# Seven quarter products for the gated up-projections, with weight sums on GpSimd

## The chip, the core and the metric

One core of one Trainium2 chip runs the whole program. Its engines have a queue each: TensorE multiplies and accumulates in PSUM, VectorE, ScalarE and GpSimd work element by element, and SyncE issues the transfers from HBM. The metric is the time of one execution on the device in microseconds; smaller is better.

## The reference

Two transformer blocks follow each other on one sequence of 512 tokens with 1024 features. The second block, which the change concerns, has two layers, and each layer is

```python
x = _layer_norm(alpha * x + 0.5 * _swiglu(x, ffn_w_gu[l, 0], ffn_w_down[l, 0]), ln_g[l, 0], ln_b[l, 0])
mix = _token_mixers(x, ...)            # four attentions side by side
x = _layer_norm(alpha * x + mix, ln_g[l, 1], ln_b[l, 1])
x = _layer_norm(alpha * x + 0.5 * _swiglu(x, ffn_w_gu[l, 1], ffn_w_down[l, 1]), ln_g[l, 2], ln_b[l, 2])

def _swiglu(h, w_gu, w_down):
    gate, up = jnp.split(h @ w_gu, 2, axis=-1)   # 1024 -> 2 x 2816
    return (jax.nn.silu(gate) * up) @ w_down     # 2816 -> 1024
```

All of it is in float32. There are four such feed-forwards, and each has 2816 / 128 = 22 "gated units": 128 gate features with the 128 up features that they multiply.

## The kernel before

Activations lie with features on the partitions: x is eight tiles of 128 features by 512 tokens (names h or x). Every operand of a product is kept as two float32r parts, a high part, which ScalarE rounds, and a low part, which VectorE gets as the difference (split, lines 406 to 409; load_split, lines 386 to 404, for weights that stream in). mm3 (lines 419 to 423) makes one 128x128 block's product as three matmuls: high by high, high by low, low by high.

swiglu works in two halves of 11 units. Of each unit it takes the gate and then the up features: proj loads 128x1024 weights, splits them in two pieces of 512 columns, and mac runs 8 x 3 matmuls over all 512 tokens into one bank. evac (line 853 on) puts SiLU of the gate into sg, multiplies it with the up product and splits the result into mid. After each half eight products over the 11 tiles of mid go down again to 1024 features and are added to x; those of the second half lie in out_norm, which also normalises.

out_norm makes the last two feature blocks by halves of the tokens. The left half's statistics, mean and normalisation run beside the right half's products. The right half's run as self.tail between the first products of the next stage: stats (the reductions, 1/std by GpSimd at line 479, and the subtraction of the mean at line 808, four tiles on VectorE and four on GpSimd), then norm for eight tiles (lines 815 to 822). chunks lets the next stage begin with four sources that take the left half of the tokens alone, so with 256 columns.

The tile framework draws up the order of each engine's queue when the program is built, with priority by program order: a weight split is queued as soon as its buffers come free, ahead of earlier code that still waits. Weights have three raw tiles (tag wr) and two pairs of parts (tags wh, wl). The working banks of PSUM are two each of tags acc, s and t, and one o.

## Time and profile before

| | |
|---|---|
| runs of the kernel, us | 3460.77, 3419.64, 3463.23 (median 3460.77) |
| span of the profiled execution, us | 3418.7 |
| the profiled execution's own time, us | 3419.64 (the run that its span fits, 0.9 around it) |
| TensorE busy | 3343.1 us, 98% |
| VectorE / ScalarE / GpSimd busy | 55% / 41% / 10% |
| mean granted TensorE clock | 0.993 |
| read from HBM | 280.20 MB, 83 GB/s |

A profile row of an engine counts an instruction from its start to its end. Matmuls overlap in the array (one of 512 columns lasts about 395 ns, and the next starts before it ends), so their pace is read from how many fit into a stretch. A window lists an instruction in every stretch that it touches. VectorE's rows overlap a little, too. A granted clock of 1.00 is 2.4 GHz, 0.5 is 1.2 GHz.

### The profile page before, as it was taken

What the parts mean: (1) busy time and instruction counts of PE and PEld (TensorE: products, weight loads), DVE (VectorE), ACT (ScalarE), POOL (GpSimd) and SP (SyncE); (2) the same over time, 40 slices, a digit from 0 to 9 for tenths busy, and PEclk for the clock granted to TensorE, in tenths of its full rate; (3) what the DMA queues carried; (4) which work ended last, traced back from release to release, by engine and by line L of the source; (5) the groups of instructions that cost most, each with busy time, mean ns of one, the idle gap of its engine ahead of it and who ended that gap; (6) DMA issues with size and microseconds to landing.
All of it is one profiled execution on the core that took longest, in us unless ns stands there. A gap on an engine that the chain in (4) does not pass through costs nothing.

```text
span 3418.7 us, 41218 instructions
## 1 busy us (share of the span) xinstructions
PE 3343.1 (98%) x15718; PEld 2681.8 (78%) x15718; DVE 1893.4 (55%) x3378; ACT 1388.7 (41%) x2680; POOL 343.0 (10%) x287
## 2 busy tenths in 40 slices
PE   8999999999999999999999999999999999999998
PEld 6776888887788888888867788888888877788887
DVE  7855564658674655344578843335333467863334
ACT  6322442436342443223466642224222356752233
POOL 3101110113110110000200100002000210010002
PEclk9999999999999999999999999999999999999999
DMA  3211223232223223232312222322232312122322
GB/s 119 88 51 48 88 91 100 89 109 68 87 94 97 93 86 99 88 102 85 108 56 65 67 81 85 101 89 90 86 103 92 112 59 78 33 89 86 105 89 78
DMA packets 105685, 293.35 MB, mean 86 GB/s; under 512 B 20752, under 2 KB 35344, under 8 KB 105232
## 3 DMA queue, kind: packets, MB, share of 16 engines
q1 hardware_dynamic: 105488, 290.73, 26.8%
q8 instruction: 123, 2.02, 0.2%
q14 instruction: 74, 0.61, 0.1%
HBM read 280.20 MB, written 2.62 MB: 83 GB/s over the span
## 4 chain that ended last, share of the span: by engine, by line
PE 84%; DVE 8%; issue 3%; ACT 2%; POOL 1%; DMA 0%; SPq 0%; ACTq 0%; DVEq 0%; POOLq 0%
PE psacc L421 15%; PE psacc L422 15%; PE psacc L423 15%; PE pss L421 5%; PE pss L423 4%; PE pss L422 4%; PE pst L421 4%; PE pst L422 4%; PE pst L423 4%; PE pso L421 2%; PE pso L423 2%; PE pso L422 2%; PE pst L1384 1%; DVE wl L403 1%; PE pso L1394 1%
## 5 line engine op out<-in xcount | busy, mean ns | idle before, releaser
L402 ACT ACTIVATE wh<-wr 128x512 fp32r<-128x512 f32 (+1 forms) x1008 | 587.5, 616 | 1301.3 <-PE psacc L422 452.1
L403 DVE TENSOR_TENSOR wl<-wr,wh 128x512 fp32r<-128x512 f32 (+1 forms) x1008 | 671.7, 692 | 653.0 <-ACT wh L402 643.4
L421 PE MATMUL psacc<-xh,wh 128*128 128x512 f32 (+1 forms) x1800 | 711.3, 396 | 10.4 <-ACT wh L402 7.8
L423 PE MATMUL psacc<-xh,wl 128*128 128x512 f32 (+1 forms) x1800 | 708.3, 394 | 10.0 <-DVE wl L403 10.0
L422 PE MATMUL psacc<-xl,wh 128*128 128x512 f32 (+1 forms) x1800 | 709.1, 394 | 2.8 <-DVE xl L523 2.4
L423 PEld LDWEIGHTS psacc<-xh,wl 128*128 128x128 f32 x1800 | 342.1, 190 | 90.8 <-DVE wl L403 13.0
L421 PEld LDWEIGHTS psacc<-xh,wh 128*128 128x128 f32 x1800 | 341.5, 190 | 91.4 <-ACT wh L402 9.6
L422 PEld LDWEIGHTS psacc<-xl,wh 128*128 128x128 f32 x1800 | 341.9, 190 | 80.7 <-DVE xl L523 5.6
L421 PE MATMUL psacc<-ph,wh 128*128 128x512 f32 x775 | 308.3, 398 | 4.6 <-DVE pl L409 2.0
L423 PE MATMUL psacc<-ph,wl 128*128 128x512 f32 x775 | 307.6, 397 | 2.4 <-DVE wl L403 2.4
L422 PE MATMUL psacc<-pl,wh 128*128 128x512 f32 x775 | 306.7, 396 | 0.1
L421 PEld LDWEIGHTS psacc<-ph,wh 128*128 128x128 f32 x775 | 145.8, 188 | 40.6 <-PE pss L423 2.8
L423 PEld LDWEIGHTS psacc<-ph,wl 128*128 128x128 f32 x775 | 145.9, 188 | 36.5 <-DVE wl L403 2.8
L422 PEld LDWEIGHTS psacc<-pl,wh 128*128 128x128 f32 x775 | 145.9, 188 | 33.8 <-DVE pl L409 0.9
L421 PE MATMUL pst<-xh,wh 128*128 128x512 f32 (+1 forms) x408 | 155.8, 384 | 4.2 <-ACT xh L818 4.2
L422 PE MATMUL pst<-xl,wh 128*128 128x512 f32 (+1 forms) x408 | 156.2, 385 | 0.2 <-DVE xl L819 0.2
L423 PE MATMUL pst<-xh,wl 128*128 128x512 f32 (+1 forms) x408 | 155.4, 383 | 0.0
L421 PE MATMUL pss<-xh,wh 128*128 128x512 f32 x392 | 155.1, 396 | 0.0
L422 PE MATMUL pss<-xl,wh 128*128 128x512 f32 x392 | 155.0, 395 | 0.0
L423 PE MATMUL pss<-xh,wl 128*128 128x512 f32 x392 | 155.0, 395 | 0.0
L577 DVE SCALAR_TENSOR_TENSOR cv<-u,vecs,cv 128x510 f32<-128x510 f32 (+1 forms) x176 | 131.1, 749 | 5.2 <-ACT cv L575 2.3
L586 POOL TENSOR_TENSOR cv<-cv,cv 128x512 f32<-128x512 f32 x44 | 57.3, 1302 | 542.7 <-DVE cv L577 517.6
(434 smaller groups left out, 5473.3 us busy)
## 6 DMA issues: line engine op xcount, KB each, us to landing
wr<-wg SPq DMA_DIRECT2D x176, 512.0 KB, 3.5
wr<-wu SPq DMA_DIRECT2D x88, 512.0 KB, 3.5
wr<-we SPq DMA_DIRECT2D x64, 512.0 KB, 3.5
wr<-wd SPq DMA_DIRECT2D x32, 512.0 KB, 3.4
wr<-we SPq DMA_DIRECT2D x64, 192.0 KB, 2.3
wr<-wi SPq DMA_DIRECT2D x22, 512.0 KB, 3.8
wr<-w_ret SPq DMA_DIRECT2D x16, 512.0 KB, 3.6
wr<-wl_in SPq DMA_DIRECT2D x16, 512.0 KB, 3.6
```

Of the source, the lines that this page charges most:

```text
L402: nc.scalar.activation(hi[:, a:b], raw[:, a:b], AF.Copy)
L403: nc.vector.tensor_tensor(lo[:, a:b], raw[:, a:b], hi[:, a:b].bitcast(F32), op=ALU.subtract)
L421: nc.tensor.matmul(ps, wh, xh, start=start, stop=False)
L422: nc.tensor.matmul(ps, wh, xl, start=False, stop=False)
L423: nc.tensor.matmul(ps, wl, xh, start=False, stop=stop)
L577: nc.vector.scalar_tensor_tensor(out=e[:, s:], in0=u[:, : T - s], scalar=self.v(f"fcw{l}{2 - s}", ch), in1=e[:, s:], op0=ALU.mult, op1=ALU ...
L586: nc.gpsimd.tensor_tensor(gate[:], gate[:], val[:], op=ALU.mult)
L1384: nc.tensor.transpose(pt[:, qb * P : (qb + 1) * P], t[:, kb * P - k0 : (kb + 1) * P - k0], self.ident)
L1394: nc.tensor.matmul(acc[0:64, q], v[:, kb, 0:64], lo[:, q], start=False, stop=False)
```

## The change

Weights and tokens of a unit are cut into quarters: gate and up rows by two halves of the 1024 input features (a11, a12, a21, a22), and x by the same halves of features and by left and right tokens (b11, b12, b21, b22). In place of eight quarter products, seven are formed from sums of quarters. Each is 4 blocks x 3 matmuls of 256 columns (prod), and R and Q accumulate several of them.

- Strassen holds the three quarters of X that are used plain ("11", "21", "22") and four sums of quarters (d, t3, t4, nf). combine makes the sums, for feature tiles j and j + 4 at a time, with four GpSimd operations of 256 columns, and splits them. out_norm's tail calls it in four rounds.
- strassen_w loads the gate and up rows of a unit and forms four sums of 512 columns on GpSimd (p1 to p4); the split is done in pieces of 1024 columns (twice or three times) and one of 512. Its raw sums (tag wc) have two tiles, which combine also uses.
- gated runs a unit's products, shifted against the unit before by the calls of next in swiglu. Evictions: e1, e2, e3 by ScalarE, combinations by VectorE, the product of gate and up by GpSimd.
- The first six units (NFIRST) of a feed-forward run the products "11" and "12" first, on the left tokens alone. Later they load their weights again for the other five products (first=False), and e2 and e3 are then formed by VectorE.
- The 22 units come in parts of 8, 8 and 6 in place of 11 and 11, so down-projections run in three parts.
- normed takes the place of rms_in for the first feed-forward of the block (its X1 is the left half only, and finish makes the rest).
- X's tiles are paired (x4), and new double tiles (xs, six) take over half of the attentions' m tiles. out_norm's late weights lie in wh2 and wl2, or in xs. load_split, weights and mm3 pass tags and a keyword on. Comments are dropped throughout.

```diff
+PARTS = ((0, 8), (8, 16), (16, 22))
+NFIRST = 6
...
+class Strassen:
+    def __init__(self, p):
+        self.p = p
+        self.parts = {n: (p.x4(), p.x4()) for n in ("11", "21", "22")}
+        self.sums = [(p.x4(), p.x4()) if j == 0 else (p.x4("xs"), p.x4("xs")) for j in range(4)]
+    def __getitem__(self, name):
+        if name in self.parts:
+            return [tuple(t[:, j * H : j * H + H] for t in self.parts[name]) for j in range(4)]
+        i = ("d", "t3", "t4", "nf").index(name)
+        return [tuple(t[:, i * H : i * H + H] for t in self.sums[j]) for j in range(4)]
+    def block(self, k, t):
+        name = f"{k // 4 + 1}{t + 1}"
+        return self[name][k % 4] if name in self.parts else None
+    def combine(self, j, x):
+        nc, p = self.p.nc, self.p
+        b11, b12, b21, b22 = (x[k][:, c] for k in (j, j + 4) for c in HALVES)
+        raw = p.pool.tile([P, 2 * T], F32, tag="wc", name=p.nm("wc"), bufs=2)
+        d, t3, t4, f = (raw[:, i * H : i * H + H] for i in range(4))
+        nc.gpsimd.tensor_tensor(t3, b22, b12, op=ALU.subtract)
+        nc.gpsimd.tensor_tensor(f, t3, b11, op=ALU.add)
+        nc.gpsimd.tensor_tensor(d, b11, b12, op=ALU.subtract)
+        nc.gpsimd.tensor_tensor(t4, f, b21, op=ALU.subtract)
+        hi, lo = self.sums[j]
+        n = 3 * H
+        nc.scalar.activation(hi[:, n:], f, AF.Copy, scale=-1.0)
+        nc.vector.scalar_tensor_tensor(
+            out=lo[:, n:], in0=f, scalar=-1.0, in1=hi[:, n:].bitcast(F32), op0=ALU.mult, op1=ALU.subtract
+        )
+        p.split(raw[:, :n], hi[:, :n], lo[:, :n])
...
+            if form == "strassen":
+                for j in range(4):
+                    norm(HALVES[1], f, (j, j + 4))
+                    X.combine(j, x)
+                    yield
+                return
...
+        def finish(bc):
+            for j in range(4):
+                for k in (j, j + 4):
+                    nc.vector.scalar_tensor_tensor(
+                        out=h[k][:], in0=h[k][:], scalar=self.v(gain, k), in1=bc[:], op0=ALU.mult, op1=ALU.mult
+                    )
+                    for t in range(2):
+                        if pair := X.block(k, t):
+                            self.split(h[k][:, t * H : t * H + H], *pair)
+                X.combine(j, h)
+                yield
...
+    def strassen_w(self, sa, sb, first=True):
+        nc = self.nc
+        out = {}
+        def put(names, src, tags, bufs=2, pool=None):
+            n = len(names) * 512
+            hi, lo = ((pool or self.pool).tile([P, n], F32R, tag=t, name=self.nm(t), bufs=bufs) for t in tags)
+            self.split(src, hi[:], lo[:])
+            for i, name in enumerate(names):
+                out[name] = [
+                    (hi[:, c : c + P], lo[:, c : c + P]) for c in range(i * 512, i * 512 + 512, P)
+                ]
+        ra = self.raw(sa, 1024)
+        if first:
+            put(("11", "12"), ra[:], ("wh", "wl"), pool=self.main)
+        if sb is None:
+            return out
+        rb = self.pool.tile([P, 1024], F32, tag="wr2", name=self.nm("wr2"), bufs=2)
+        nc.sync.dma_start(rb[:], sb)
+        a11, a12, a21, a22 = ra[:, :512], ra[:, 512:], rb[:, :512], rb[:, 512:]
+        c1, c2 = (self.pool.tile([P, 1024], F32, tag="wc", name=self.nm("wc"), bufs=2) for _ in range(2))
+        p2, p1, p3, p4 = c1[:, :512], c1[:, 512:], c2[:, :512], c2[:, 512:]
+        nc.gpsimd.tensor_tensor(p1, a21, a22, op=ALU.add)
+        nc.gpsimd.tensor_tensor(p2, p1, a11, op=ALU.add)
+        put(("p2", "p1"), c1[:], ("wh", "wl"), pool=self.main)
+        nc.gpsimd.tensor_tensor(p3, a11, a21, op=ALU.add)
+        nc.gpsimd.tensor_tensor(p4, p2, a12, op=ALU.add)
+        put(("p3", "p4"), c2[:], ("wh2", "wl2"))
+        put(("22",), a22, ("wh3", "wl3"), 1)
+        return out
+    def prod(self, ps, W, X, start):
+        for j in range(4):
+            self.mm3(ps[:, :H], *W[j], *X[j], start and j == 0, j == 3, skip_group_check=True)
+    def scratch(self):
+        return [self.pool.tile([P, T], F32, tag="m", name=self.nm("g"), bufs=self.bufs["m"]) for _ in range(2)]
+    def gated(self, X, srcs, mid, tags, sent=None):
+        nc = self.nc
+        tr, tq, tz = tags
+        gv, hv = sent or self.scratch()
+        g1, g2, e1, n2 = gv[:, :H], gv[:, H:], hv[:, :H], hv[:, H:]
+        silu = lambda t: nc.scalar.activation(t, t, AF.Silu)
+        if sent is None:
+            W = self.strassen_w(*srcs)
+            R = self.pt(tag=next(tr))
+            self.prod(R, W["11"], X["11"], True)
+            nc.scalar.copy(e1, R[:, :H])
+            yield
+            Z = self.pt(tag=next(tz))
+            self.prod(Z, W["12"], X["21"], True)
+            nc.vector.tensor_tensor(g1, e1, Z[:, :H], op=ALU.add)
+            silu(g1)
+            yield
+        else:
+            W = self.strassen_w(*srcs, first=False)
+            R = self.pt(tag=next(tr))
+        e2, e3 = (self.pool.tile([P, H], F32, tag="u", name=self.nm("u"), bufs=3)[:] for _ in range(2))
+        def out(t):
+            if sent is None:
+                nc.scalar.copy(t, R[:, :H])
+            else:
+                nc.vector.tensor_tensor(t, e1, R[:, :H], op=ALU.add)
+        self.prod(R, W["p2"], X["nf"], sent is not None)
+        out(e2)
+        yield
+        Q = self.pt(tag=next(tq))
+        self.prod(Q, W["p1"], X["d"], True)
+        yield
+        self.prod(R, W["p3"], X["t3"], False)
+        out(e3)
+        nc.vector.scalar_tensor_tensor(out=n2, in0=e3, scalar=-1.0, in1=Q[:, :H], op0=ALU.mult, op1=ALU.subtract)
+        yield
+        self.prod(R, W["22"], X["t4"], False)
+        if sent is None:
+            last = R[:, :H]
+        else:
+            nc.vector.tensor_tensor(e1, e1, R[:, :H], op=ALU.add)
+            last = e1
+        nc.vector.scalar_tensor_tensor(out=g1, in0=last, scalar=-1.0, in1=g1, op0=ALU.mult, op1=ALU.mult)
+        yield
+        self.prod(Q, W["p4"], X["22"], False)
+        nc.vector.tensor_tensor(g2, e2, Q[:, :H], op=ALU.add)
+        silu(g2)
+        nc.gpsimd.tensor_tensor(g2, g2, n2, op=ALU.mult)
+        pair = self.xpair("m")
+        self.split(gv[:], pair[0][:], pair[1][:])
+        mid.append(pair)
...
+            if n1:
+                if normed is not None:
+                    X1, X, scale, finish = normed
+                    left, right = X1[:4], X1[4:]
                 else:
+                    left, right = X["11"], X["21"]
+                held = []
+                def done(W, R, gv):
+                    self.prod(R, W["12"], right, False)
+                    if bc is None:
+                        nc.scalar.activation(gv[:, :H], R[:, :H], AF.Silu)
+                    else:
+                        nc.vector.tensor_tensor(gv[:, :H], R[:, :H], bc[:, :H], op=ALU.mult)
+                        nc.scalar.activation(gv[:, :H], gv[:, :H], AF.Silu)
+                for j in range(n1):
+                    W = self.strassen_w(wg[a + j], None)
+                    R = self.pt(tag=next(around))
+                    self.prod(R, W["11"], left, True)
+                    if normed is not None and j == 0:
+                        bc = scale()
+                        self.tail = finish(bc)
+                    gv, hv = self.scratch()
+                    early.append((gv, hv))
+                    if bc is None:
+                        nc.scalar.copy(hv[:, :H], R[:, :H])
+                    else:
+                        nc.vector.tensor_tensor(hv[:, :H], R[:, :H], bc[:, :H], op=ALU.mult)
+                    held.append((W, R, gv))
+                    if j > 0:
+                        done(*held.pop(0))
+                    next(self.tail, None)
+                done(*held.pop(0))
+                for _ in self.tail:
+                    pass
+            before = None
+            for j in range(a, b):
+                sent = early[j - a] if j - a < n1 else None
+                g = self.gated(X, (wg[j], wg[FC + j]), mid, tags, sent)
+                next(g)
+                if before:
+                    next(before)
+                next(g)
+                if before:
+                    next(before, None)
+                for _ in range(1 if sent else 3):
+                    next(g)
+                before = g
+            for _ in before:
+                pass
...
-                    ps = self.proj(I[f"we{l}{s}"][nb][:, : HF * P], mid, HF)
+                    ps = self.proj(I[f"we{l}{s}"][nb][:, a * P : b * P], mid, b - a)
...
-        return self.phase(name, None, m=38, e=6)
+        return self.phase(name, None, m=20)
...
-        return self.phase(name, None, m=24, v=8, pt=4, e=5, y=4, p1=1)
+        return self.phase(name, None, m=12, v=8, pt=4, e=5, y=4, p1=1)
```

## Rows read from the trace of the kernel before

**Rows 1.** The page's first part: busy us (share of the span) and instructions.
```profile
span 3418.7 us, 41218 instructions
PE 3343.1 (98%) x15718; PEld 2681.8 (78%) x15718; DVE 1893.4 (55%) x3378; ACT 1388.7 (41%) x2680; POOL 343.0 (10%) x287
```
**Rows 2.** The page's chain that ended last, shares of the span by engine.
```profile
PE 84%; DVE 8%; issue 3%; ACT 2%; POOL 1%; DMA 0%; SPq 0%; ACTq 0%; DVEq 0%; POOLq 0%
```
**Rows 3.** Windows: steady up-projection, unbroken 256 columns, and a transition between stages.
```profile
core 0: us, PE busy (x) PEld busy (x) DVE busy (x) ACT busy (x) POOL busy (x), PEclk, DMA share, GB/s
1480.00:1580.00 100.00, 100.00 (x430) 80.55 (x430) 44.28 (x70) 30.56 (x53) 0.00 (x0) 1.00 0.29 95
1687.00:1695.00 8.00, 8.00 (x70) 8.00 (x70) 2.08 (x3) 4.61 (x10) 0.00 (x0) 1.00 0.40 131
1965.00:1988.00 23.00, 20.83 (x159) 19.98 (x158) 21.64 (x51) 18.20 (x43) 4.50 (x5) 0.93 0.15 46
```
**Rows 4.** Lines by form, ScalarE and VectorE: busy us, mean ns, idle before.
```profile
L402 ACT ACTIVATE wh<-wr 128x512 fp32r<-128x512 f32 x920 | 541.3, 625 | 1198.0 <-PE psacc L422 410.5 <-issue 404.6 <-PE pss L422 149.2
L408 ACT ACTIVATE ph<-sg 128x512 fp32r<-128x512 f32 x90 | 56.1, 623 | 36.9 <-DVE sg L869 30.3 <-DVE sg L1282 4.4 <-DVE sg L1280 2.1
L774 ACT ACTIVATE sq<-h 128x256 f32<-128x256 f32 x32 | 13.0, 412 | 27.3 <-DVE h L739 27.3
L1450 ACT COPY y<-psacc 128x256 f32<-128x256 f32 x12 | 4.4, 363 | 6.9 <-PE psacc L423 6.9
...
L409 DVE TENSOR_TENSOR pl<-sg,ph 128x512 fp32r<-128x512 f32 x90 | 62.0, 689 | 11.2 <-ACT ph L408 10.2
L409 DVE TENSOR_TENSOR pl<-sg,ph 128x256 fp32r<-128x256 f32 x12 | 5.0, 419 | 2.1 <-ACT ph L408 2.1
L739 DVE SCALAR_TENSOR_TENSOR h<-psacc,h 128x256 f32<-128x256 f32 x14 | 5.8, 416 | 5.5 <-PE psacc L423 5.5
```
**Rows 5.** Lines by form, GpSimd: its commonest operation on 512 columns.
```profile
L586 POOL TENSOR_TENSOR cv<-cv,cv 128x512 f32<-128x512 f32 x44 | 57.3, 1302 | 542.7 <-DVE cv L577 517.6 <-ACT cv L585 25.1
```
**Rows 6.** Line 808 on both engines: ns min/median/max, first and last start us.
```profile
L808 DVE TENSOR_TENSOR h<-h,bc x48: 424/954/987, 1660.0 to 3410.4; 128x256 f32<-128x256 f32 x48
L808 POOL TENSOR_TENSOR h<-h,bc x48: 731/916/981, 1660.2 to 3411.0; 128x256 f32<-128x256 f32 x48
```
**Rows 7.** Timeline: start us, us; two low parts with GpSimd's operation, two without.
```profile
413.58 2.38 DVE L403 TENSOR_TENSOR wl<-wr,wh 128x512 fp32r<-128x512 f32 x2
413.84 1.58 POOL L586 TENSOR_TENSOR cv<-cv,cv 128x512 f32<-128x512 f32 x1 [3.11 <-DVE cv L577]
...
1309.70 1.29 DVE L403 TENSOR_TENSOR wl<-wr,wh 128x512 fp32r<-128x512 f32 x2 [4.76 <-ACT wh L402]
```
**Rows 8.** Timeline of VectorE and GpSimd around the subtraction of the mean.
```profile
1660.04 3.06 DVE L808 TENSOR_TENSOR h<-h,bc 128x256 f32<-128x256 f32 x4 [0.59 <-ACT bc L805]
1663.02 1.25 DVE L815 SCALAR_TENSOR_TENSOR h<-h,vecs,pso 128x256 f32<-128x256 f32 x3
1660.20 3.48 POOL L808 TENSOR_TENSOR h<-h,bc 128x256 f32<-128x256 f32 x4
```
**Rows 9.** Timeline of a transition, attentions to feed-forward: TensorE and VectorE.
```profile
1965.58 0.28 PE L421 MATMUL psacc<-xh,wh 128*128 128x256 f32 x1
1981.94 0.51 PE L421 MATMUL pst<-xh,wh 128*128 128x256 f32 x2 [2.14 <-ACT xh L818]
1977.00 3.61 DVE L808 TENSOR_TENSOR h<-h,bc 128x256 f32<-128x256 f32 x4
1986.72 0.88 DVE L819 SCALAR_TENSOR_TENSOR xl<-h,vecs,xh 128x256 fp32r<-128x256 f32 x2
```
**Rows 10.** The page's DMA issues: count, KB each, us to landing.
```profile
wr<-wg SPq DMA_DIRECT2D x176, 512.0 KB, 3.5
wr<-we SPq DMA_DIRECT2D x64, 512.0 KB, 3.5
wr<-we SPq DMA_DIRECT2D x64, 192.0 KB, 2.3
```

More of the change, by code (lines that the diff above doesn't have):

```diff
@@ L509, in rms_in @@
         X, tot = [], self.bct()
-        sqs = [tot] + [self.main.tile([P, T], F32, tag="x", name=self.nm("sq"), bufs=16) for _ in range(KC - 2)] + [self.bct()]
+        sqs = [tot]
+        for _ in range(KC // 2 - 1):
+            t = self.x4(dt=F32)
+            sqs += [t[:, :T], t[:, T:]]
+        sqs.append(self.bct())
         for k in range(KC):
@@ L725, in total, with out_norm @@
         return t
-    def out_norm(self, x, src, Y, c, l, s, late=2, out=None):
+    def out_norm(self, x, src, Y, c, l, s, late=2, out=None, form="plain", wtag="m"):
         nc = self.nc
@@ L762, in out_norm @@
             s1 = self.total(s1, x[nb], nc.gpsimd if self.around else nc.vector)
-        W = [self.weights(src(nb), nk, "m") for nb in range(E, KC)]
-        X = [] if out is not None else [self.xpair() for _ in range(KC)]
+        W = [self.weights(src(nb), nk, wtag) for nb in range(E, KC)]
+        X = [self.xpair() for _ in range(KC)] if form == "plain" else Strassen(self) if form == "strassen" else None
         def products(cols, tags):
@@ L815, in norm @@
                 nc.vector.scalar_tensor_tensor(out=xs, in0=xs, scalar=g, in1=f, op0=ALU.mult, op1=ALU.mult)
-                if out is None:
-                    hi, lo = X[k][0][:, cols], X[k][1][:, cols]
+                pair = None
+                if form == "plain":
+                    pair = X[k][0][:, cols], X[k][1][:, cols]
+                elif form == "strassen":
+                    pair = X.block(k, cols.start // H)
+                if pair is not None:
+                    hi, lo = pair
                     nc.scalar.activation(hi, xs, AF.Identity, bias=b)
@@ L1515, in mixers, with stack @@
         wo = I[f"wo{l}"]
-        def stack(src, order, name):
-            out = [self.t(name, F32R, "m") for _ in range(4)]
+        def stack(src, order, name, pair):
+            if pair == 0:
+                out = [t for _ in range(2) for t in self.xpair("xs")]
+            else:
+                out = [self.t(name, F32R, "m") for _ in range(4)]
             for b in range(4):
```

134 lines of the change are left out of this document (74 added, 60 removed).

## The prediction

> **What bounds the kernel now.** I read the busy table first: TensorE is busy for 98% of the 3418.7 us span, VectorE for 55%, ScalarE for 41%, GpSimd for 10% [rows 1]. The chain that ended last confirms it: 84% of it is TensorE's [rows 2]. So time falls only where TensorE gets less to do, and only while nothing else starves it.
>
> Next the windows, for what one product costs. In 100 us of steady up-projection 430 products of 512 columns are listed [rows 3]; some two were already under way at the edge, so 428 steps, 0.2336 us each. In 8 us of unbroken 256-column products the same count gives 68 steps, 0.1176 us each, although every product also loads its weights: half the columns take half the time. Both stretches ran at the full 2.4 GHz (granted clock 1.00). VectorE was busy for 44% of the long stretch, ScalarE for 31%, GpSimd not at all. That empty GpSimd column is what the change wants to use.
>
> **TensorE's part.** A gated unit (gate and up features of one 128-wide block) has 48 products of 512 columns now: 48 x 0.2336 = 11.21 us. Seven quarter products of 4 x 3 matmuls of 256 columns are 84 x 0.1176 = 9.88 us, 1.33 us less. There are 4 feed-forwards of 22 units, 88 units: at most 117 us, 3.4% of the span. I take this as certain. The price is that the operands of five of the seven are sums.
>
> **What each full unit adds elsewhere**, by the durations in [rows 4] (a 1024-element operation extrapolated by the step from 256 to 512):
> - ScalarE: high parts of the weights 3 x 1.05 + 0.63, three PSUM copies of 0.36, two SiLU of about 0.41, one high part of 0.62: 6.3 us in 9.88. Enough room.
> - VectorE: low parts 3 x 1.23 + 0.69, four combinations of 256 columns at 0.42, one low part of 0.69: 6.7 us. Enough room on its own.
> - GpSimd: four sums of 128x512 at 1.30 [rows 5] and a 256-column product at 0.73 (the shortest in [rows 6]): 5.9 us. Enough room on its own.
>
> But VectorE and GpSimd are not alone. Two low parts take 1.29 us when GpSimd is idle and 2.38 when one GpSimd sum of 512 starts behind them; the sum takes 1.58 in place of about 1.3 [rows 7]. So a GpSimd sum holds VectorE off for 1.09 us. VectorE operations with one input in PSUM do not suffer: three of them took 1.25 us beside GpSimd's fourth subtraction [rows 8]. Low parts have both inputs in SBUF and do suffer. In [rows 8] four 256-column subtractions on each engine proceed in turns, one pair per 0.88 us (3.48 / 4 = 0.87). The part of an operation that excludes the other is its slope: 0.27 us per 256 elements on VectorE, 0.55 on GpSimd (half of 1.09); their sum 0.82 leaves 0.06 to pass the turn.
>
> For a full unit that makes one shared resource: GpSimd 4 x 1.09 + 0.55 = 4.9 us, VectorE 4096 two-SBUF elements = 16 x 0.27 = 4.3, five changes of turn 0.3: 9.5 us. TensorE needs 9.88. They nearly tie; the four PSUM combinations must wait in VectorE's queue behind blocked low parts, and the weight sums have only one unit of buffers to run ahead (tag wc, two tiles per unit). Bounds: 9.88 (all hidden) and 11.0 (the two engines' whole instructions in turn: 3 x 1.23 + 2 x 0.69 + 5.93). Nearest is the turn-taking of [rows 8], so I take 10.1. There are 16 full units per feed-forward: 16 x (10.1 - 11.21) = -17.8 us.
>
> In [rows 8] a pair of 256-column operations whose whole instructions excluded each other would take 0.42 + 0.73 = 1.15 us; 0.88 was measured. A rule of the Trainium skill speaks against this change: "SBUF — State Buffer", section "SBUF: two separate sides", has the port pair that the two engines share as an exclusive lock, which an operation with two SBUF inputs holds for its whole length. The trace agrees on the exclusion and differs on its length; by the Trainium skill's rule the sum would be that of rival 2 below, 3497 in place of 3402.
>
> **The first six units of each feed-forward (NFIRST) are dearer.** Their two plain products use the left half of the tokens alone, 6 x 24 x 0.1176 = 16.9 us, while the right half is still being normalised. The remaining five products per unit then take 60 x 0.1176 = 7.06 us of TensorE, but carry all four sums: GpSimd 4.9, VectorE 3328 two-SBUF elements 3.5, turns 0.3: 8.7 us. Here the shared resource is the bound. Its evictions also move from ScalarE to VectorE (tensor_tensor with e1), and the eviction of the third sum stands in VectorE's queue behind low parts while the next product into that bank waits. I take 9.0; bounds 7.06 and 10.2 (whole instructions: 4.3 + 5.9).
>
> How late is the right half? Before, in the transition behind the attentions, the next stage begins at 1965.58, the subtraction of the mean ends 15.0 us later (1977.00 + 3.61), the normalisation at 1987.6, and TensorE waits 2.14 us for it [rows 9]. The change adds, behind the subtraction, four rounds (tail, combine), each of four GpSimd sums of 256 and about five 256-element portions of two-SBUF VectorE work: 4 x 0.88 + 0.3 = 3.8 us; plus 1.4 to the first sum and 1.9 for the last parts. All of X's sums stand 15.0 + 1.4 + 15.2 + 1.9 = 33.5 us after the stage began. TensorE has 16.9 us to do, and can use the first sums (nf of j = 0) before the last exist. It also spends part of the transition at 1.2 GHz (0.93 granted over 23 us, [rows 3], about 1.6 us lost). I take 10 us of waiting; bounds 3 (rounds overlap better) and 14 (sums of X complete before the first use). The weight sums share tag wc with these rounds, and so cannot go far ahead.
>
> Six first units: 16.9 + 10 + 6 x 9.0 = 80.9 us, against 6 x 11.21 + 2.1 = 69.4: +11.5 us. The case with normed differs in detail (four rounds behind scale), and I price it alike.
>
> **Small parts.** Parts of 8, 8 and 6 units end three times in place of two; at an end the product into R waits for an eviction with nothing between, 0.36 plus a queue: some 2 us per feed-forward in all, between 0 and 4. One more accumulation into x is 8 VectorE operations of 0.69 beside down products of 24 x 0.2336 = 5.6 us, whose own VectorE work is 2.1: hidden. Loads: 50 + 24 of 512 KB or less in place of 44 + 32 per feed-forward, landing in 3.5 us [rows 10], with three raw tiles in advance: hidden; if not, up to 3.5 us once per part. SyncE gets no more to issue. In the attentions only the place of tiles changes (24 narrow ones become 12 and 6 double ones): nothing, or a few us if a tile comes free late.
>
> **Sum.** Per feed-forward -17.8 + 11.5 + 2 = -4.3 us, four times -17. The profiled run is 3419.6 us (span 3418.7 and 0.9 around it); it is the shortest of three, and the median shown is 3460.8, 41 above. On the profiled run's footing: 3419.6 - 17 = 3402.
>
> **Rivals.**
> 1. GpSimd's sums hide: full unit 9.9, first units 7.6, waiting 4. Per feed-forward 16 x (-1.31) + (16.9 + 4 + 45.6 - 69.4) + 1 = -23, so 3328. For it: each engine alone has a third of its time free. Against: 8.7 us of turns in the first units.
> 2. Slower: the two engines' whole instructions exclude each other, at the upper bounds above. Full unit 11.0, first units 10.2, waiting 12: -3.4 + (16.9 + 12 + 61.2 - 69.4) + 2 = +19, so 3497. It turns the change into a loss over 2% from about 17 us per feed-forward, a full unit of 10.9. For it: VectorE's subtractions stretched to 0.95 us, from 0.42 [rows 6]. Against: the 0.88 us pairs. (The Trainium skill's page named above has this as its rule.)
> 3. As forecast, but TensorE's waits bring spells of 1.2 GHz: at 1.6 us each, some 30 of them (one per first unit and more) give 3450. For it: transitions are where the granted clock drops now. Against: the waits within units should be short.
> That 256-column products cost more than half, so that nothing is saved, would need 11.21 / 84 = 0.133 us; the trace shows 0.118.
>
> **Numbers.** Forecast 0.58, rival 1 0.20, rival 2 0.15, rival 3 0.07. Over 2% is about what a measurement of this kernel can tell from no change: below 3351 or above 3488. Rival 1 is faster, rival 2 slower, the rest the same: 0.20, 0.65, 0.15. The likeliest case's own range is 3365 to 3445; the range that leaves out 2 in 10 reaches to both rivals, 3330 to 3490, and so holds the 41 us between the runs too.
>
> **What would show it.** Products of 256 columns 0.118 us apart in full units; low parts of 1024 elements stretched from 1.23 to above 2 us wherever GpSimd works; TensorE waiting some 10 us per feed-forward for X's sums, mostly on VectorE's low parts, and then for p2 and p3 weights in the first units; period 10.1 in full units and 9.0 in first ones. I am wrong if full units run at 9.9 with GpSimd busy 60% (rival 1), at 11 with VectorE always busy (rival 2), or if the clock reads below 0.95 in steady stretches (rival 3).

## The result: 3.5% slower, and the profile after

The changed kernel took 3559.2 us (median; 3535.4 to 3581.3), the kernel before in the same runs 3442.3 (3419.6 to 3463.2): ratio 1.0351, 95% interval 1.0264 to 1.0437. The forecast was 3402, its range ended at 3490.

The runs of both kernels scatter by some 40 us, and the profiled run of after, unlike that of before, has a spell of 99 us at 1.2 GHz from 238 us on (third line of the three windows further down), in the first block, which the change leaves alone, so that its second block begins 42.7 us later. From here on I compare the **second block**, from its first load of wg to the end of the span.

The first load's time, before and after (operation, count, issue time min/median/max in ns, first and last start in us):

```profile
L399 SPq DMA_DIRECT2D wr<-wg x170: 327/328/337, 1276.6 to 3312.3; - x170
```
```profile
L435 SPq DMA_DIRECT2D wr<-wg x112: 327/328/372, 1319.3 to 3474.4; - x112
```
Before, 3418.7 - 1276.6 = 2142.1 us; after, 3576.5 - 1319.3 = 2257.2: 115 us more. From the first load of one stage to that of the next, the four feed-forwards cost 42, 25, 23 and 27 us more, the attentions between them 1.5 us less in sum. The loss is in the feed-forwards alone.

The busy table and the chain that ended last, after (before: [rows 1, 2]):

```profile
span 3576.5 us, 48384 instructions
PE 3374.1 (94%) x18478; PEld 2826.0 (79%) x18478; DVE 2358.4 (66%) x3710; ACT 1616.7 (45%) x2998; POOL 1034.0 (29%) x791
...
PE 63%; DVE 15%; POOL 8%; issue 6%; ACT 5%; DMA 2%; SPq 0%; POOLq 0%; ACTq 0%; DVEq 0%
```
TensorE's share of the span fell from 98 to 94%, and it holds 63% of the chain where it held 84%. These lines cover the whole execution, the spell in the first block too. The second block alone, before and then after (start and end, length, busy us and instructions of each engine, granted clock, DMA share, GB/s):

```profile
1276.60:3418.70 2142.10, 2108.96 (x10229) 1710.73 (x10227) 1092.73 (x2107) 859.45 (x1772) 151.10 (x135) 0.99 0.27 85
1319.30:3576.50 2257.20, 2093.75 (x12989) 1831.76 (x12987) 1562.45 (x2444) 1095.03 (x2100) 847.44 (x643) 0.96 0.28 86
```
TensorE's idle time rose from 33 to 163 us. Its busy time fell by 15 us only, where the fewer columns would make 117, and the clock records of the second block have 198 us at 1.2 GHz where they had 37. So it waits, and it works at the low clock. Where, three more windows show; in order: first part of the second feed-forward, its second part, and the spell in the first block:

```profile
2045.80:2175.40 129.60, 99.70 (x669) 93.70 (x668) 85.89 (x129) 60.71 (x106) 77.34 (x62) 0.86 0.30 94
2223.30:2302.00 78.70, 77.66 (x648) 76.32 (x647) 64.33 (x69) 46.78 (x78) 47.62 (x34) 1.00 0.34 101
240.00:360.00 120.00, 116.86 (x360) 66.36 (x359) 40.57 (x88) 18.89 (x48) 10.62 (x9) 0.60 0.05 18
```
Each stretch of parts one and two holds 648 of the part's 672 up-products; the last 24 share 3.8 us with the first down products. The second part is what was forecast. The first takes 129.6 us for matmuls that at 0.1176 us make 669 x 0.1176 = 78.7: TensorE idles 29.9 us and is busy 99.7 - 78.7 = 21 us longer than at full pace; the granted clock of 0.86 explains some 18 of them (0.14 x 129.6). The first parts of the other three feed-forwards take 137.6, 127.4 and 130.3 us. What TensorE waited for in the first window (us in total, times, longest; the five costliest of twelve):

```profile
PE psacc L475 <- DVE u L1030: 7.6, 6, 2.3
PE pst L475 <- ACT wh L458: 4.2, 2, 2.5
PE psacc L477 <- DVE wl L459: 4.2, 5, 1.1
PE pso L549 <- POOL f L533: 3.6, 1, 3.6
PE psacc L475 <- ACT u L1028: 3.1, 1, 3.1
```
No single wait is long: evictions (L1030, L1028), high parts (L458), low parts (L459), GpSimd's 1/std (L533). Behind most of them, as the experiments will show, stand GpSimd's sums. Its timeline (start, duration), from the last round of X's sums (L329 to L332) into the weight sums of the first three units (L980 to L984):

```profile
2079.32 0.83 POOL L329 TENSOR_TENSOR wc<-h,h 128x256 f32<-128x256 f32 x1 [1.17 <-ACT h L885]
2080.12 1.27 POOL L980 TENSOR_TENSOR wc<-wr 128x512 f32<-128x512 f32 x1
2081.35 0.73 POOL L330 TENSOR_TENSOR wc<-wc,h 128x256 f32<-128x256 f32 x1
2082.04 1.28 POOL L981 TENSOR_TENSOR wc<-wc,wr 128x512 f32<-128x512 f32 x1
2083.28 0.91 POOL L332 TENSOR_TENSOR wc<-wc,h 128x256 f32<-128x256 f32 x1
2086.13 1.29 POOL L983 TENSOR_TENSOR wc<-wr,wr 128x512 f32<-128x512 f32 x1 [1.95 <-DVE xs L459]
2087.38 2.27 POOL L984 TENSOR_TENSOR wc<-wc,wr 128x512 f32<-128x512 f32 x1
2089.72 1.29 POOL L980 TENSOR_TENSOR wc<-wr 128x512 f32<-128x512 f32 x1
2091.09 2.14 POOL L981 TENSOR_TENSOR wc<-wc,wr 128x512 f32<-128x512 f32 x1
2093.19 1.29 POOL L983 TENSOR_TENSOR wc<-wr,wr 128x512 f32<-128x512 f32 x1
2094.44 2.29 POOL L984 TENSOR_TENSOR wc<-wc,wr 128x512 f32<-128x512 f32 x1
2096.80 1.26 POOL L980 TENSOR_TENSOR wc<-wr 128x512 f32<-128x512 f32 x1
```
VectorE's low parts beside them:

```profile
2085.09 0.96 DVE L459 TENSOR_TENSOR xs<-wc,xs 128x768 fp32r<-128x768 f32 x1 [1.49 <-ACT xs L458]
2086.58 1.92 DVE L459 TENSOR_TENSOR wl<-wc,wh 128x1024 fp32r<-128x1024 f32 x1 [0.53 <-ACT wh L458]
2090.77 1.32 DVE L459 TENSOR_TENSOR wl<-wc,wh 128x1024 fp32r<-128x1024 f32 x1 [2.27 <-ACT wh L458]
```
Three things are to be seen. The stage began at 2045.8 and X's last sum was split at 2085.09 + 0.96 = 2086.05, 40.3 us later. The first unit's weight sums stand in GpSimd's queue among and behind X's, and the last of them (L984) ends at 2089.65. From there a unit's four sums take 2096.80 - 2089.72 = 7.08 us, in turn with VectorE; that holds for the first three units only. GpSimd's product of gate and up, one per unit, gives the pace:

```profile
L1053 POOL TENSOR_TENSOR g<-g,g x6: 1188/1192/1477, 2107.8 to 2162.5; 128x256 f32<-128x256 f32 x6
```
The first of the six units reaches it 2107.8 - 2045.8 = 62.0 us into the stage, the sixth 54.7 us later: a **start of 62.0** and a **period of 10.9 us**. The forecast put them at 16.9 + 10 + 9.0 = 35.9 and 9.0. Start and period are what the experiments are read by.

Between the last of the first unit's sums (2089.65) and its product of gate and up (2107.8) lie 18 us. The chain of waits ends them so (start, duration, what; "..." stands for the 23 products between):

```profile
2097.84 1.30 DVE wl L459
2099.15 0.34 DVE u L1030
2099.53 0.58 PE psacc L475
2100.12 0.22 PE psacc L476
...
2105.22 0.12 PE pss L477
```
The first unit's third sum is taken out of PSUM (u, L1030) only at 2099.15. It stands in VectorE's queue behind a low part of the second unit, and that one waited for the second unit's last GpSimd sum (2094.44 + 2.29). Then products come at 1.2 GHz: from 2100.12 on 24 of them take 5.10 us, 2.3 us more than at 0.1176. Between 2059.5 and 2162.6 us the chain holds no products but those from 2099.53 to 2106.3; the rest of it is GpSimd, ScalarE, VectorE and loads.

### The profile page after: what moved, and what is told of

It reads as the page before. It is cut to its first block, busy times and chain, and to the rows that moved or that the text cites. A ratio compares the mean times of both kernels' runs of the same rounds, so it can differ in the third digit from the quotient of the medians.

```text
span 3576.5 us, 48384 instructions
## 1 busy us (share of the span) xinstructions
PE 3374.1 (94%) x18478; PEld 2826.0 (79%) x18478; DVE 2358.4 (66%) x3710; ACT 1616.7 (45%) x2998; POOL 1034.0 (29%) x791
## 4 chain that ended last, share of the span: by engine, by line
PE 63%; DVE 15%; POOL 8%; issue 6%; ACT 5%; DMA 2%; SPq 0%; POOLq 0%; ACTq 0%; DVEq 0%
PE psacc L475 14%; PE psacc L476 14%; PE psacc L477 14%; DVE wl L459 5%; PE pss L475 3%; PE pss L476 2%; PE pss L477 2%; DMA wr<-wg 2%; PE pst L475 2%; PE pst L476 2%; PE pst L477 1%; DVE wl L453 1%; PE pst L1627 1%; POOL wc L981 1%; POOL g L1053 1%
## 5 line engine op out<-in xcount | busy, mean ns | idle before, releaser
L475 PE MATMUL psacc<-xq,wh 128*128 128x512 f32 (+1 forms) x1952 | 735.7, 378 | 67.4 <-DVE u L1030 24.4
L477 PE MATMUL psacc<-xq,wl 128*128 128x512 f32 (+1 forms) x1952 | 717.5, 368 | 23.0 <-DVE wl L459 14.1
L476 PE MATMUL psacc<-xq,wh 128*128 128x512 f32 (+1 forms) x1952 | 717.4, 368 | 3.7 <-DVE xq L581 2.0
L452 ACT ACTIVATE wh<-wr 128x512 fp32r<-128x512 f32 (+2 forms) x692 | 395.3, 610 | 629.7 <-PE psacc L476 346.3
L453 DVE TENSOR_TENSOR wl<-wr,wh 128x512 fp32r<-128x512 f32 (+2 forms) x692 | 508.5, 766 | 186.2 <-ACT wh L452 173.3
L475 PEld LDWEIGHTS psacc<-xq,wh 128*128 128x128 f32 x1952 | 375.7, 193 | 157.9 <-ACT u L1028 33.3
L477 PEld LDWEIGHTS psacc<-xq,wl 128*128 128x128 f32 x1952 | 376.4, 193 | 92.4 <-DVE wl L459 17.7
L476 PEld LDWEIGHTS psacc<-xq,wh 128*128 128x128 f32 x1952 | 376.9, 193 | 68.6 <-DVE xq L581 5.4
L459 DVE TENSOR_TENSOR wl<-wc,wh 128x1024 fp32r<-128x1024 f32 x176 | 255.4, 1452 | 105.4 <-ACT wh L458 105.1
L475 PE MATMUL psacc<-ph,wh 128*128 128x512 f32 (+1 forms) x796 | 313.4, 394 | 4.8 <-DVE xs L459 2.2
L477 PE MATMUL psacc<-ph,wl 128*128 128x512 f32 (+1 forms) x796 | 312.9, 394 | 2.6 <-DVE wl L453 2.6
L476 PE MATMUL psacc<-pl,wh 128*128 128x512 f32 (+1 forms) x796 | 312.5, 393 | 0.0
L458 ACT ACTIVATE wh<-wc 128x1024 fp32r<-128x1024 f32 x176 | 185.6, 1055 | 218.1 <-POOL wc L981 86.9
L459 DVE TENSOR_TENSOR wl<-wr,wh 128x1024 fp32r<-128x1024 f32 (+1 forms) x176 | 251.6, 1430 | 17.2 <-ACT wh L458 15.6
L475 PE MATMUL psacc<-xs,wh 128*128 128x256 f32 (+1 forms) x824 | 244.6, 297 | 0.0
L476 PE MATMUL psacc<-xs,wh 128*128 128x256 f32 (+1 forms) x824 | 244.0, 296 | 0.0
L458 ACT ACTIVATE wh<-wr 128x1024 fp32r<-128x1024 f32 (+1 forms) x176 | 148.5, 844 | 171.9 <-PE psacc L476 104.3
```

The source lines that it names most:

```text
L452: nc.scalar.activation(hi[:, a:b], raw[:, a:b], AF.Copy)
L453: nc.vector.tensor_tensor(lo[:, a:b], raw[:, a:b], hi[:, a:b].bitcast(F32), op=ALU.subtract)
L458: nc.scalar.activation(hi, src, AF.Copy)
L459: nc.vector.tensor_tensor(lo, src, hi.bitcast(F32), op=ALU.subtract)
L475: nc.tensor.matmul(ps, wh, xh, start=start, stop=False, **kw)
L476: nc.tensor.matmul(ps, wh, xl, start=False, stop=False, **kw)
```

## The experiments

All are edits of the changed kernel. Columns: second block, then start, period and length (648 products) of the first part of the second feed-forward, in us, all from the traces. Each row is one profiled execution, so I make nothing of a difference of one or two us.

| kernel | second block | start | period | length |
|---|---|---|---|---|
| before | 2142.1 | | | |
| after | 2257.2 | 62.0 | 10.9 | 129.6 |
| e1 product g*u on VectorE | 2241.6 | 64.4 | 10.8 | 129.5 |
| e2 no weight sums in first units | 2173.2 | 52.1 | 8.6 | 106.8 |
| e3 no sums of X | 2224.0 | 51.5 | 11.1 | 119.8 |
| f1 neither | 2146.1 | 46.1 | 8.6 | 102.2 |
| f2 these weight sums on VectorE | 2197.1 | 52.6 | 9.9 | 113.5 |
| g2 f2, X's sums on VectorE | 2196.8 | 51.2 | 9.9 | 112.2 |
| g3 g2, product g*u on VectorE | 2177.4 | 51.6 | 9.2 | 110.6 |
| e5 third tile for raw up rows | 2237.0 | 64.6 | 9.7 | 124.9 |
| e6 second tile for quarter 22 | 2237.9 | 64.0 | 9.4 | 122.7 |
| e7 down loads last | 2249.8 | 61.4 | 10.8 | 126.8 |
| e4 fill, one place | 2300.1 | 68.8 | 11.7 | 140.7 |
| g1 fill, five places | 2286.8 | 66.3 | 11.7 | 136.3 |
| h1, h2, h3: first part by whole products | 2144.0, 2124.0, 2108.7 | | | |

**e1. GpSimd's queue order.** GpSimd waits for ScalarE's SiLU before its product, and the next unit's weight sums stand behind it.
```
-        nc.gpsimd.tensor_tensor(g2, g2, n2, op=ALU.mult)
+        nc.vector.tensor_tensor(g2, g2, n2, op=ALU.mult)
```


> One edit to the changed kernel: the product of gate and up (last line of gated's GpSimd work, 256 columns per unit) runs on VectorE, so GpSimd's queue holds nothing but sums. Theory A (a loop through GpSimd's queue): in the first units that product stands ahead of the next unit's sums and waits for the end of the unit before, so sums, splits, products and the product of gate and up follow one another, which makes the 11 us per first unit. Then the period falls to about 9 us, the first part of the second feed-forward (133 us from its first up product to steady down products) to some 118, and the whole by about 60 us. Theory B (only the taking of turns between VectorE and GpSimd over SBUF): the same elements have two SBUF inputs on VectorE too, so period and time stay within 1 us and 15 us. Theory C (the granted clock is the cause and the waits are short without it): no change either.

The first parts hardly moved; the second and third lost 1.7 and 1.4 us each, and their full units now come 9.9 us apart in place of 10.3. That wait is not what sets the first part.

**e2, e3, f1. The sums taken away.** e2 leaves out the weight sums of the six first units and splits raw quarters in their place; e3 leaves out X's sums (plain parts instead); f1 both. Products, splits and evictions stay (one split of X of 768 columns becomes two, of 512 and 256). All three leave out sums that the result needs.
```
+        if first:
+            nc.gpsimd.tensor_tensor(p1, a21, a22, op=ALU.add)
...
-        put(("p2", "p1"), c1[:], ("wh", "wl"), pool=self.main)
+        put(("p2", "p1"), c1[:] if first else rb[:], ("wh", "wl"), pool=self.main)
```


> The four GpSimd sums of weights are left out in the first six units of each feed-forward: raw weights are split in their place (same number and size of splits and products; this part of the result is not the reference's). Theory A and theory B both: a first unit falls from 11 us to about TensorE's 7.1 to 7.6, the first part from 133 to some 100 us, the whole by 100 to 130 us, to about the time of the kernel before. If it is the late sums of X that count and not those of the weights: the first part stays above 120 us and the whole falls by less than 50.

> The four sums of quarters of X are left out in combine (X's own quarters are split in their place; nothing after that is the reference's), so the rounds in the tail have no GpSimd work, and all weight sums stay. If the late X is what starves TensorE: X's parts stand some 10 us sooner (30 in place of 40 us after the stage begins), and with the clock the whole falls by 40 to 80 us. If the weight sums set the pace from the start (theories A and B): the wait only moves to the weights of the first unit, and the whole falls by less than 30 us; the period of 11 us per first unit stays.

> Leaves out both: the weight sums of the six first units (the raw quarters are split in their place) and X's sums (plain parts in their place); all products, splits and evictions stay, the full units too. If the two are separate shares, their gains add: 84 + 33 = 117 us off the second block, 2257 -> 2140, first parts near 97 us, with 79 us of products. If they are one share, GpSimd's time, seen twice, the gain is hardly above the 84 of the weight sums alone: 2165 to 2175, first parts of 104 to 107, and what is left is ScalarE's and VectorE's evictions and splits.

84, 33 and 111 us: the shares nearly add (117). The weight sums account for the period's fall from 10.9 to 8.6 (7.1 to 7.6 was expected) and for 10 us of the start, X's sums for the start only. Together they are worth 111 of the 115 us lost; that takes in the low clock that came with them, which falls from 198 to 97 us in f1's second block. But without any sum the first part still takes this:

```profile
2022.40:2124.60 102.20, 89.69 (x668) 86.19 (x668) 78.29 (x133) 59.59 (x110) 27.40 (x22) 0.92 0.37 119
```
that is 46 us of start and 8.6 per unit, where TensorE needs 7.06, so the first part eats what the full units save. What is left there, to go by the code, is evictions and splits in small pieces one after another; no run takes those away, so that is not shown.

**f2, g2, g3. The sums on VectorE.** The same sums, then X's, then the product too.
```
-        nc.gpsimd.tensor_tensor(p1, a21, a22, op=ALU.add)
+        eng = nc.gpsimd if first else nc.vector
+        eng.tensor_tensor(p1, a21, a22, op=ALU.add)
...
```


> The four weight sums of each of the six first units on VectorE instead of GpSimd; the full units as in the changed kernel. Alone a VectorE sum of 512 columns would take some 0.6 us (a low part of 512 columns takes that), against 1.3 to 2.3 on GpSimd, and four a unit add 2.4 us to VectorE's 8 or so of a unit. GpSimd's own slowness and the turns between the two engines set the period: units fall from 11 to 8.5 to 9.5 us, first parts from 130 to 112 to 120, second block 2200 +- 20. VectorE's load sets the period (its splits and evictions, to which the sums are now added): first parts stay or grow, 130 to 140, second block 2255 to 2300.

> X's sums on VectorE too, beside the weight sums of the six first units (second block 2197 us with these alone). X's 16 sums of 256 columns a feed-forward are some 16 x 0.42 = 6.7 us on VectorE. GpSimd's slowness is what X's share is: most of the 33 us come back, second block 2170 to 2185, first parts 106 to 110. Additional VectorE work on the transition's path costs what the faster sums give: 2190 to 2210.

> As before, and the product of gate and up on VectorE too: GpSimd then has only the sums of the full units. In the changed kernel that product's move was worth 15.6 us, all of it in the second and third parts, and nothing in the first: 2155 to 2172 if it is the same here. If it is the last of GpSimd's work in the first part that holds it, more: down to 2145. A seven-product first part stays above the 2109 us of the version whose first part is made of eight products.

f2 won 60 of the 84 us, although VectorE was already the second busiest engine. In f2 a sum of 512 takes VectorE this long (mean ns), in the changed kernel GpSimd that long:

```profile
L982 DVE TENSOR_TENSOR wc<-wc,wr 128x512 f32<-128x512 f32 x24 | 18.4, 765 | 0.1
L984 DVE TENSOR_TENSOR wc<-wr,wr 128x512 f32<-128x512 f32 x24 | 16.4, 685 | 0.1
```
```profile
L984 POOL TENSOR_TENSOR wc<-wc,wr 128x512 f32<-128x512 f32 x88 | 150.4, 1710 | 1.6
L981 POOL TENSOR_TENSOR wc<-wc,wr 128x512 f32<-128x512 f32 x88 | 137.9, 1567 | 165.5 <-DMA wr<-wg 161.0
```
A sum on GpSimd holds VectorE off for 1.09 us [rows 7], longer than the 0.69 to 0.77 that VectorE needs to make it. g2 won nothing more: whichever of the two engines makes X's sums, the time is the same. g3 won 19, most of it e1's 16; 25 to 42 were expected.

**e5, e6, e7. Buffers and the load order.** The chain of waits between 2085 and 2165 us runs in a loop: low part of quarter 22, load of the next up rows into the tile that it frees, GpSimd's sums, ScalarE's and VectorE's splits. One lap of it in the changed kernel (pieces of 0.10 us and less left out; the two called "issue" are VectorE's low parts, still running):

```profile
2115.87 0.68 DVE wl L459
2116.57 4.13 DMA wr<-wg
2120.87 1.27 POOL wc L980
2122.14 1.24 POOL wc L983
2123.38 1.45 POOL wc L981
2124.84 1.07 ACT wh L458
2125.97 1.22 issue
2127.19 0.25 DVE wl L459
2127.44 0.35 issue
2127.90 4.51 DMA wr<-wg
```
From load to load that is 2127.90 - 2116.57 = 11.3 us: 4.3 of load, 4.0 of three sums, the rest splits. No product of TensorE is on it.
```
-        rb = self.pool.tile([P, 1024], F32, tag="wr2", name=self.nm("wr2"), bufs=2)
+        rb = self.pool.tile([P, 1024], F32, tag="wr2", name=self.nm("wr2"), bufs=3)
...
-        put(("22",), a22, ("wh3", "wl3"), 1)
+        put(("22",), a22, ("wh3", "wl3"), 2)
```
The first pair of lines is e5, the second e6; each takes two tiles of tag m (20 to 18) to make room. e7 issues the down-projection's loads behind the last load of up rows.

> The changed kernel with three raw tiles in place of two for the up rows (wr2), and 18 m tiles in place of 20 to make room. Theory D (raw weights come too late): in the first units the up rows' tile is released only by the split of quarter 22, which stands in ScalarE's queue behind the split of the weight sums, and the next load takes 4.4 us from there to GpSimd's first sum; load, sums, split and split of 22 follow one another, about 11 us. With a third tile a first unit takes 8 to 9 us (GpSimd's own 6.5 to 8 with turns), the first part of the second feed-forward falls from 133 to about 115 us, the whole by 60 to 90. Theory B (turns between VectorE and GpSimd set the 11 us): nothing changes, within 15 us. If 18 m tiles hurt, parts two and three (78.7 and 58.5 us) grow.

> The changed kernel with two tiles in place of one for the parts of quarter 22 (wh3, wl3), 18 m tiles. Theory D: the split of 22 no longer waits for the product of 22 of the unit before, so the raw tile is free sooner; about the same gain as with a third raw tile, 40 to 90 us, if ScalarE's queue order does not hold it anyway. Theory B: nothing changes.

> The changed kernel with the loads of the down-projections of the first two parts put behind the part's last load of up rows in SyncE's queue (order alone). Theory E: loads for the down-projections stand in SyncE's queue ahead of the next unit's up rows and wait there for a raw tile that GpSimd's last sum releases (19.9 us of SyncE's waiting between 2085 and 2165): then the last three first units gain some 2 us each and the whole 20 to 40 us. Theory D: these waits end at about the same time as that for the raw tile of the up rows, so nothing is gained (within 10 us), and the down-projections may start late.

The tiles shorten the period by 1.2 and 1.5 us and lengthen the start by 2 to 3: 20 us each, where 40 to 90 were expected; the load order is worth 7. So the loop is real, but opening it at one place does not bring 9.0. No run opens both places at once.

**e4, g1. The clock.** Products of 512 columns into a bank that nobody reads: 12 a unit behind the product with p1 (e4), or 3 ahead of each of a unit's five products (g1; these lines are g1's).
```
+        o = self.pt(tag="o")
+        for k in range(FILL):
+            nc.tensor.matmul(o[:], self.filler[:, :P], self.filler, start=k == 0, stop=k == FILL - 1)
```


> Twelve more products of 512 columns in each of the six first units, into a sum of their own that nobody reads, behind the product with p1: 12 x 0.234 = 2.8 us of TensorE's time a unit at full clock, 16.8 us a first part. They fill part of its idle time. The clock is a cause: with the gaps filled the low clock of the second block (200 us in the changed kernel) falls under 60 us, the half-speed products no longer hold back the loop over evictions and splits, the six units come every 9 to 10 us instead of 11, and the second block takes 2180 to 2220 us instead of 2257. The clock is only the mark of a period that VectorE, GpSimd and ScalarE set: the low clock falls as much, the units still come every 11 us, and the second block stays at 2245 to 2275. TensorE is itself the bound of the first part: the fill is paid in full, 4 x 16.8 = 67 us more, 2325.

> Three more products of 512 columns ahead of each of the five products of a first unit, from operands that are always ready, into a sum that nobody reads: 15 x 0.234 = 3.5 us a unit, 21 us a first part, put into the very gaps. The clock is a cause: the low clock of the second block falls from 200 us to under 80, TensorE's 20 us a first part lost at 1.2 GHz come back, and the fill lies in the 30 us of idle time: first parts 115 to 125 us for 130, second block 2200 to 2240 us beside 2257. The clock is only the mark: the low clock falls, but the first parts stay at 128 to 135. The fill is paid for, as the one of 2.8 us was to two thirds (43 of 67 us): first parts 140 or more, second block over 2300; then TensorE's time counts in the loop, and its gaps cannot be filled for nothing.

e4 does not answer: TensorE's time at 1.2 GHz in the second block only fell from 198 to 174 us. In g1 it fell to 140, and between the first and the sixth unit of the second feed-forward from 10.2 to 3.4 us, yet the period rose, from 10.9 to 11.7. Of the 84 us put in, 30 were paid for. By itself this does not acquit the clock, because the fill stands in the units' own way and may cost what the clock gives back. e6 settles it without a fill: from the first to the sixth product of gate and up, its first feed-forward and its second take

```profile
1368.60:1415.40 46.80, 38.98 (x298) 37.97 (x299) 37.33 (x51) 19.39 (x28) 32.27 (x24) 0.93 0.32 96
2067.80:2115.00 47.20, 36.62 (x298) 35.61 (x299) 36.34 (x51) 19.39 (x28) 32.66 (x24) 1.00 0.31 96
```
the same 9.4 us a unit, at a granted clock of 0.93 and of 1.00 (the third takes 9.7 at 0.89, the fourth 9.4 at 0.96). So within the six units the low clock is the mark of the gaps and not what sets the pace. In the start of the second feed-forward 24 of its 62 us are at 1.2 GHz, and the chain has 2.3 us lost to it.

**h1, h2, h3. Seven products only where the operands have long been ready.** The first part of each feed-forward (8 units) by whole products of 512 columns, as before; parts two and three by seven quarter products; X's sums are made during the first part; h3 also has e1's edit. (In h1 one group of X's sums lies over tiles still in use, so its products have wrong operands and TensorE waits for it; h2 makes that group later.)
```
+                self.chunks(srcs, X.plain, evac, 4 if scale is None else 0, 2 if scale is not None else 0)
...
+            for j in range(a, b) if not n1 else ():
```


> The first part of each feed-forward (8 units) by eight quarter products as in the kernel before, the other 14 units by seven; the sums of X are made meanwhile, and the weight sums have no first units to serve. By the full units' measured 10.2 us against 11.2: 14 x 1.0 x 4 = 57 us less than the kernel before, so about 3365 on the footing of its profiled run, and TensorE's waits at the transitions as in the kernel before. If the seven-product form costs elsewhere than in the first units (more storage traffic, longer queues), the gain is under 20 us.

> As h1_first_plain, with X's last group of sums made behind the first part's products (h1 made it before, in tiles that those products still read: TensorE waited 19.7 us for it, and the products used wrong operands). The first part falls from 109 us to about 92 (8 plain units at 11.2 and the transition's waits of the kernel before), parts two and three stay at 82 and 62 us with their last products. Whole: 14 x 1.0 x 4 = 57 us less than the kernel before, some 3365 on the footing of its profiled run, if the seven-product form is worth in its full units what the trace of the changed kernel shows there; no gain if the first units were not the whole loss.

> The second version: first part of each feed-forward by eight whole products as in the kernel before, the other two parts by seven products with their sums on GpSimd, and the product of gate and up on VectorE instead of GpSimd. The last gated unit of a part ends 3.7 us ahead of the down products in the version with GpSimd's product (a gap of that length at the end of both parts); the step on VectorE takes some 0.5 us for 1.1. Expected: gap of 2.5 to 3 us, parts 2 and 3 shorter by 1.5 us each as in the changed kernel, 4 x 2 x 1.5 = 12 us, 3403 beside 3442 before, ratio 0.993 to the kernel before, where the version with GpSimd's product had 0.9964. If VectorE's queue at the parts' ends holds the step up (it comes behind a split of 0.7 to 1.5 us), nothing is won: 0.996 to 0.998.

h1: 3439.3 us, ratio to the kernel before 1.0053 (1.0006 to 1.0100). h2: 3414.8, 0.9964 (0.9907 to 1.0022). h3: 3419.5 (3385.3 to 3434.4), 0.9971 (0.9932 to 1.0011). h1 is a little slower than before (its interval just leaves out 1); h2 and h3 cannot be told from no change by their times. In the profiled runs h3 is ahead of before by 2142.1 - 2108.7 = 33 us in the second block, one execution of each. What I expected of h3 on the gaps of 3.7 us was a misreading: they hold a part's last 24 products, with TensorE busy throughout, and they stayed; the two parts shortened by 1.4 us or so each. Expected of h2 were 3365; its profiled span is 3402.4, and some 30 of the missing 37 us lie in the three first parts that begin behind another stage, 100 to 105 us long where 92 were expected. In h3 the second feed-forward's takes

```profile
1954.00:2055.50 101.50, 95.99 (x500) 81.66 (x501) 56.62 (x104) 46.21 (x96) 20.39 (x22) 0.97 0.27 87
```
for eight units that make 8 x 11.21 = 89.7 us: 5.5 us idle, and the rest products outside the up-projection and at 1.2 GHz.

## Why the prediction was wrong

**Right: TensorE's part and the full unit.** 648 products of 256 columns in 78.7 us at granted clock 1.00. Eight units with the 24 shared products took 81.8 us, 10.2 each, where 10.1 was forecast; GpSimd busy for 47.62 / 78.70 = 61%, forecast 5.9 of 9.88. TensorE lost about 1 us to waits there. The 14 units of parts two and three brought about the gain priced: the second feed-forward lost 25 us, its first part alone 133.4 - (8 x 11.21 + 2.1) = 42, so the rest gained 17, where 14 x 1.11 less 2 were priced. At the ends of parts TensorE stays busy.

**Right: the price of a turn.** L983 ends at 2087.42, the low part beside it at 2088.50, 1.08 us later, where the whole operation was priced at 1.23 from [rows 4]. L984 ends 1.15 us after that, alone 1.3. The forecast had 1.08 and 1.09 from [rows 7, 8].

By the Trainium skill ("SBUF — State Buffer", section "SBUF: two separate sides") the lock holds for the whole instruction; these rows bear it out to about nine tenths of each operation. "Perfetto Trace Analysis", section "Optimizing Scalar/DVE Operations", of the same Trainium skill says that moving work between VectorE and GpSimd might not help because of the shared port; the trace agrees, and f2 shows more: taking the sums back to VectorE gained 60 us.

**Wrong: "Six first units: 16.9 + 10 + 6 x 9.0 = 80.9".** With two full units that is 101.1 us for the first part. Measured from 2045.8 to its last product, 133.4: 32 us too little. Four times that is nearly the whole error (115 lost, 17 forecast as gained). Two steps of it failed; they make 36 us, of which the two full units behind them took back some 4. A third term, the clock, was far off but hardly counts:

1. *The start, 26 of the 32 us.* X's sums came at 40.3, not 33.5. Worse, I wrote that the weight sums "cannot go far ahead" and gave it no price: GpSimd works its queue in order, and the first unit's sums were done only 3.6 us behind X's last. I let TensorE resume at 26.9 us, on weight sums that GpSimd began at 34.3 (2080.12). And 9.0 is a pace; a first unit's splits, five products and evictions follow one another, two units interleaved, and took from 2089.65 to 2107.81, 18 us. I had named the third sum's eviction behind low parts and left 0.3 us for it. f1, without sums, starts at 46: 16 of the 26 us go with the sums, and what makes the other 10 is not shown.
2. *The period, 10.9 for 9.0.* I took the busiest shared resource, 8.7 us of turns, as the pace. But GpSimd is busy for only 35.2 of the 54.7 us between the first and the sixth unit. With so few tiles the pace is a loop through the load, GpSimd, ScalarE and VectorE: faster sums (f2), another raw tile (e5), another tile of parts (e6) each shorten it by 1.0 to 1.5 us, and none to 9.0. I had put the loads at nothing, "with three raw tiles in advance"; the up rows have two of their own (wr2), and their load is 4.3 of the lap's 11.3 us. Both bounds I gave were sums of busy time, so the truth lay above the upper one, 10.2.
3. *The clock.* I noted 1.6 us lost to it in a transition and gave it no term; the first parts had 38 to 48 us at 1.2 GHz each. Rival 3 had named the place (the first units) and priced 30 spells at 48 us; the 198 us at half speed could cost twice that. But in the six units of e6 the clock makes no difference, and in the start the chain has 2.3 us lost to it. The rest of it fell, in the second feed-forward, where nothing on the chain waited for TensorE. By these, leaving it out cost the forecast little; that was luck, for no row that I had read told it.

**The rivals.** Rival 1 (all hidden) fell. Rival 2 is nearest, with 3497 - 3420 = 77 us lost where the second block lost 115, but not for its reason alone: full units stayed at 10.2, not 11.0, and the first units passed even its 10.2. My range was too narrow because its upper end priced capacity, and no case priced latency.

## What to carry to other kernels

Before giving a helper engine the operands of the next stage, write down its queue in order across the stage's boundary and price the way of the first unit end to end; the busiest resource is the pace only where buffers let units overlap. An engine that takes turns with VectorE is no third engine: a sum goes to GpSimd only where VectorE has time to be held off. And use a trick with derived operands where they have long been ready (h3, so far one profiled execution's gain), not where the stage before has just produced the data.

## What the runs showed of the hardware

VectorE and GpSimd held each other off in both directions: a 1024-element low part stretched from 1.23 to 1.92 us behind a GpSimd sum that had 0.84 us left, and a sum of 512 from 1.29 to 2.27 behind a low part that had 1.12 left, so each by about 0.15 us less than the other's remaining time. Filling TensorE's gaps with 3.5 us of products a unit (g1) took most of the low clock out of the six units and made them no faster; in e6 the six units came every 9.4 us at a granted clock of 0.93 and at 1.00 alike.
